# Weight sums of a Strassen feed-forward block moved to VectorE in a pinned order

## The chip, the cores and the metric

The kernel runs on one core of a Trainium2 chip. Its time is the device time of one execution in microseconds (us); the number that counts is the median of several executions. The engines are named as the profile names them: PE is TensorE (PEld its weight loads), DVE is VectorE, ACT is ScalarE, POOL is GpSimd, and SP is SyncE, which here issues the transfers.

## The reference

One step of a small two-layer transformer is computed for 128 prompt rows and 512 sample rows of width 1024. Each layer has a feed-forward block, a mixer (attention in layer 0, a Fourier transform with a projection in layer 1) and a second feed-forward block. Each of the three parts normalises the rows, scales and shifts them by vectors computed from a condition, and adds its result, times a gate vector, to the stream.

```python
def _rms(x, g):
    y = xf * lax.rsqrt(jnp.mean(xf * xf, axis=-1, keepdims=True) + EPS)
    return (y * g.astype(jnp.float32)).astype(x.dtype)
def _modulate(h, shift, scale):
    return h * (1 + scale) + shift
def _swiglu(h, wg, wu, wd):                      # 1024 -> 2816 -> 1024
    return (jax.nn.silu(h @ wg) * (h @ wu)) @ wd
...
hs = _modulate(_rms(ys, norm_g[l, 2]), ms[6], ms[7])
ys = ys + 0.5 * ms[8] * _swiglu(hs, ffn_wg[l, 1], ffn_wu[l, 1], ffn_wd[l, 1])
```

## The kernel before, in words

**Arithmetic.** Everything is kept transposed, features on the 128 partitions, the 640 rows along the columns, in two halves: H=0 has 384 columns, H=1 has 256. A matrix product in float32 is made of three products of rounded parts. Each operand is split into a high half (a rounded copy) and a low half (the rest), and `mm3` adds high·high, high·low and low·high (L497, L498 and L499 in the profile). The high half of a weight is cast on ACT, the low half is a subtraction `raw - high`, on POOL (L160 for plain weights, L109 for the sums below).

**Stages.** The change touches the last feed-forward block of the program (`ffn_last`), from about 1860 us on, and the end of the Fourier stage ahead of it. The block runs over six chunks of its hidden features, `CHUNKS = (4, 4, 2, 4, 4, 4)` blocks of 128. In each chunk PE first makes gate and up of each block (one *unit* of weights, 2048 columns, in two transfers of 512 KB), then `down` multiplies the chunk's results `g` by the down weights (one unit for two blocks), 8 output tiles for each column half, and DVE adds each to the stream (L704).

**Strassen units.** Chunk 0 is plain: for each unit, gate and up on H=0 (384 columns), and on H=1. From chunk 1 on the columns are cut into two halves of 320 and a unit is computed by `seven`, seven products instead of eight. They use sums of weights (S1 to S4) and sums of inputs (T1 to T4); the weight sums are made in `load_sums`: DVE adds and subtracts (L124, L125, L128, L133), ACT casts (L113), POOL or DVE makes the low halves (L109). Between products ACT copies partial results out of PSUM (`snap`, L858) and takes a silu (L888), and DVE adds another product (L870, L883, L893) and multiplies gate and up (L862). The products write to two regions `a` and `b` of one PSUM tile, so a product into one also waits for a read of the other. Two units are interleaved; the last of a chunk ends with its products S4 and A22 alone. At the start and the end of the chunk nothing of another unit stands between the products.

**Buffers.** A unit's split weights live in a ring of three (`wpool`), the forms S2 to S4 in a pool of 12, raw weights in a pool of three. A unit's transfer, casts and sums are a small task; tasks advance on virtual time, which the kernel's author counts with `tick` as PE work is emitted. This fixes the order in which instructions are written. In the kernel before, the scheduler of the framework may then reorder each engine's instructions by its own estimate of when they are ready.

**Head of the block.** `PreNorm` normalises the input: squares (ACT), their sum over feature tiles (POOL, L519), a matmul of ones on the sum (L535), the root (POOL, L545), diagonal matrices (DVE, L552) and a matmul that spreads the factor over partitions (L557). Then for each of 8 feature tiles DVE scales (L320), ACT shifts and rounds (L323), and DVE makes the low half (L324). It is done for H=0 and then H=1. The input sums T1 to T4 follow (L342, ACT L352).

Of the kernel before, what the change touches and what calls it, by code (L numbers as in the profile page):

```python
# [21 lines left out]
KT = D // P  # L22
# [52 lines left out]
class Units:  # L75


    def __init__(self, k):
        self.k = k
        self.todo = []  # L80
        self.ready = []
        self.turn = self.served = self.live = 0

# [3 lines left out]
    def prefetch(self, n=1, eng=None):  # L87
        for _ in range(n):
            if self.todo:
                self.ready.append(self.k.spawn(self.load(*self.todo.pop(0), eng or self.k.nc.gpsimd)))  # L90

    def load_sums(self, ap, cols, eng):


        k, nc = self.k, self.k.nc
        W = UNIT // 4
        r1, r2 = k.raw(), k.raw()
# [4 lines left out]
        turn = self.turn  # L102
        self.turn += 1
        forms = {}

        def low(eng, lo, src, hi):
            for o in range(0, src.shape[1], W):
                c = slice(o, o + W)
                eng.tensor_tensor(lo[:, c], src[:, c], hi[:, c].bitcast(F32), op=ALU.subtract)  # L109

        def put(names, src, eng, at=None):
            h, l = (k.wide(k.fpool, "form", w=W) for _ in range(2)) if at is None else (hi[:, at], lo[:, at])
            nc.scalar.copy(h, src)  # L113
            low(eng, l, src, h)
            for n, name in enumerate(names):
                forms[name] = tuple(t[:, n * W : (n + 1) * W] for t in (h, l))

        yield 3500
        while self.served < turn:
            yield 300  # L120
        s1 = k.wide(k.spool2, "s1", F32, W)
        put(("A11", "A12"), r1, eng, slice(0, RAW))
        yield 500
        nc.vector.tensor_tensor(s1, r2[:, :W], r2[:, W:], op=ALU.add)  # L124
        nc.vector.tensor_tensor(r2[:, :W], r1[:, :W], r2[:, :W], op=ALU.subtract)  # L125
        yield 500
        put(("S1",), s1, eng, slice(RAW, RAW + W))
        nc.vector.tensor_tensor(s1, s1, r1[:, :W], op=ALU.subtract)  # L128
        while self.live > 1:
            yield 300  # L130
        self.live += 1
        put(("S2",), s1, nc.vector)
        nc.vector.tensor_tensor(r1[:, W:], r1[:, W:], s1, op=ALU.subtract)  # L133
        yield 700
        put(("S3",), r2[:, :W], nc.vector)
        yield 700
        put(("S4",), r1[:, W:], nc.vector)
        yield 700
        put(("A22",), r2[:, W:], eng, slice(RAW + W, UNIT))
        self.served += 1  # L140
        return forms

    def load(self, ap, cols, eng):
# [6 lines left out]
        for c in range(0, cols, RAW):  # L150
            e = min(RAW, cols - c)
            raw = self.k.raw()
            nc.sync.dma_start(raw[:, :e], ap[:, c : c + e])
            raws.append((raw, c, e))
        for i, (raw, c, e) in enumerate(raws):
            yield 1500 if i else 4000
            nc.scalar.copy(hi[:, c : c + e], raw[:, :e])  # L157
            for o in range(0, e, 512):
                w = min(512, e - o)
                eng.tensor_tensor(  # L160
                    lo[:, c + o : c + o + w],
                    raw[:, o : o + w],
                    hi[:, c + o : c + o + w].bitcast(F32),
                    op=ALU.subtract,
                )
        return hi, lo
# [100 lines left out]
class PreNorm:  # L267


    def __init__(self, k, l, i):  # L270
        self.k, self.l, self.i = k, l, i
        self.h = []
        self.acc = [None, None]
        self.task = [None, None]
        self.feeds = [None, None]
        self.open = self.free = False
        self.started = False
        self.pauses = [(2500, 3000), (9000, 3000)]
# [25 lines left out]
    def normalise(self, H):  # L304
# [4 lines left out]
        sh, sc = (k.mod[self.l][3 * self.i + j] for j in range(2))  # L309
        for d in range(KT):  # L310
            while not self.open:
                yield 200
# [4 lines left out]
            x = k.xs(d, H)  # L317
            for cols, c in k.parts(H):
                b = sh[:, d, c : c + 1]
                nc.vector.scalar_tensor_tensor(  # L320
                    t[:, cols], x[:, cols], sc[:, d, c : c + 1], r[:, cols], ALU.mult, ALU.mult
                )
# [3 lines left out]
                )  # L326
            yield 900
# [56 lines left out]
class Kern:  # L384
# [74 lines left out]
    def open_last(self):  # L459
# [4 lines left out]
        self.open_halves(8, 3, "right")  # L464
# [431 lines left out]

    def ffn_last(self, l, i, nrm, nxt, before_last):
# [5 lines left out]
        for ch, nf in enumerate(CHUNKS):  # L903
# [14 lines left out]
            else:  # L918
                gs = wide(nf)
# [20 lines left out]
            if last:  # L940
                before_last()
            for H in (0, 1) if ch == 0 or last else ("second", "first"):
# [4 lines left out]
            u.prefetch(nf // 2)  # L947
# [397 lines left out]
    def fourier(self, nrm, nxt):  # L1345
# [120 lines left out]
        def out(w, q, H):  # L1466
            n = NA if H == 0 else NB
            for j in range(2):
# [10 lines left out]
                self.add_x(ps, 2 * q + j, H, gate, nxt if H == 0 else None)  # L1479
# [13 lines left out]
        nxt.later(1)  # L1493
# [362 lines left out]
```

## Time and profile before

| what | before |
|---|---|
| median of 3 runs | 2390.07 us (2389.2 to 2391.84) |
| profiled execution, its own time | 2390.42 us |
| its span in the trace | 2388.6 us |
| mean granted PE clock | 0.983 |
| PE / DVE / ACT / POOL busy | 96% / 67% / 34% / 40% |

The span is what the trace covers; 1.8 us of the profiled execution's time lie outside it. PE is the engine that is nearly always busy. "Granted clock" is the share of the full TensorE clock that PE was given; it has two levels, 1.2 and 2.4 GHz, so that 0.50 is the lower one and a mean between says how long each held.

### The profile page before, as it was taken

What the parts mean: (1) busy time and instruction counts of PE and PEld (TensorE: products, weight loads), DVE (VectorE), ACT (ScalarE), POOL (GpSimd) and SP (SyncE); (2) the same over time, 40 slices, a digit from 0 to 9 for tenths busy, and PEclk for the clock granted to TensorE, in tenths of its full rate; (3) what the DMA queues carried; (4) which work ended last, traced back from release to release, by engine and by line L of the source; (5) the groups of instructions that cost most, each with busy time, mean ns of one, the idle gap of its engine ahead of it and who ended that gap; (6) DMA issues with size and microseconds to landing.
All of it is one profiled execution on the core that took longest, in us unless ns stands there. A gap on an engine that the chain in (4) does not pass through costs nothing. (4 is left out here: it accounts for less than half of the span.)

```text
span 2388.6 us, 38803 instructions
## 1 busy us (share of the span) xinstructions
PE 2291.5 (96%) x15518; PEld 2255.8 (94%) x15518; DVE 1595.8 (67%) x2984; ACT 815.7 (34%) x1689; POOL 947.6 (40%) x763
## 2 busy tenths in 40 slices
PE   8899999999999999999999999999999898989988
PEld 6899999998999999999999999999999798988988
DVE  5877778777777886677767767765364565465554
ACT  4222222254544522222225222222273324232433
POOL 1534433464111443343436334433355334334423
PEclk9999999999999999999999999999999799999999
DMA  8544434321111243333442443432211122121221
GB/s 297 164 133 133 150 123 143 126 75 48 41 41 45 89 132 123 126 122 117 147 137 73 132 124 124 135 121 78 67 61 55 54 71 73 54 86 54 89 71 53
DMA packets 70467, 243.90 MB, mean 102 GB/s; under 512 B 7888, under 2 KB 12688, under 8 KB 70032
## 3 DMA queue, kind: packets, MB, share of 16 engines
q1 hardware_dynamic: 70288, 241.44, 31.7%
q8 instruction: 122, 2.00, 0.3%
q14 instruction: 57, 0.47, 0.1%
HBM read 238.62 MB, written 2.79 MB: 101 GB/s over the span
## 5 line engine op out<-in xcount | busy, mean ns | idle before, releaser
L160 POOL TENSOR_TENSOR wlo<-raw,whi 128x512 fp32r<-128x512 f32 (+1 forms) x520 | 736.2, 1446 | 1081.5 <-ACT whi L157 1034.2
L157 ACT CAST whi<-raw 128x1024 fp32r<-128x1024 f32 (+1 forms) x267 | 269.7, 1036 | 515.3 <-PE t L498 244.9
L704 DVE SCALAR_TENSOR_TENSOR x<-t,mod,x 128x128 f32<-128x128 f32 (+3 forms) x696 | 277.1, 433 | 152.0 <-PE t L499 149.7
L613 DVE CUSTOM_DVE_ANT_0 junk<-wmt,crow 128x1024 f32<-128x1024 f32 x256 | 372.7, 1456 | 3.1 <-ACT crow L1580 0.6
L497 PE MATMUL s<-a,whi 128*128 128x386 f32 (+1 forms) x1056 | 359.7, 341 | 5.4 <-DVE b L740 3.4
L499 PE MATMUL s<-a,wlo 128*128 128x386 f32 (+1 forms) x1056 | 359.8, 341 | 0.1
L498 PE MATMUL s<-a,whi 128*128 128x386 f32 (+1 forms) x1056 | 358.7, 340 | 0.0
L497 PE MATMUL s<-b,whi 128*128 128x256 f32 (+1 forms) x1056 | 296.6, 281 | 0.0
L499 PE MATMUL s<-b,wlo 128*128 128x256 f32 (+1 forms) x1056 | 296.4, 281 | 0.0
L498 PE MATMUL s<-b,whi 128*128 128x256 f32 (+1 forms) x1056 | 296.4, 281 | 0.0
L497 PE MATMUL t<-a,whi 128*128 128x384 f32 (+1 forms) x792 | 270.6, 342 | 14.5 <-DVE x L704 5.3
L498 PE MATMUL t<-a,whi 128*128 128x384 f32 (+1 forms) x792 | 269.3, 340 | 0.9 <-DVE a L507 0.7
L499 PE MATMUL t<-a,wlo 128*128 128x384 f32 (+1 forms) x792 | 268.1, 339 | 0.0
L497 PE MATMUL t<-b,whi 128*128 128x256 f32 x760 | 215.4, 283 | 4.8 <-ACT b L563 2.7
L498 PE MATMUL t<-b,whi 128*128 128x256 f32 x760 | 213.8, 281 | 0.0
L499 PE MATMUL t<-b,wlo 128*128 128x256 f32 x760 | 213.8, 281 | 0.0
L497 PEld LDWEIGHTS s<-a,whi 128*128 128x128 f32 x1056 | 200.4, 190 | 6.6 <-issue 4.2
L499 PEld LDWEIGHTS s<-a,wlo 128*128 128x128 f32 x1056 | 200.2, 190 | 2.3 <-issue 1.6
L498 PEld LDWEIGHTS s<-a,whi 128*128 128x128 f32 x1056 | 200.2, 190 | 1.6 <-issue 1.2
L497 PEld LDWEIGHTS s<-b,whi 128*128 128x128 f32 x1056 | 199.1, 189 | 0.0
L498 PEld LDWEIGHTS s<-b,whi 128*128 128x128 f32 x1056 | 198.9, 188 | 0.0
L499 PEld LDWEIGHTS s<-b,wlo 128*128 128x128 f32 x1056 | 198.8, 188 | 0.0
(294 smaller groups left out, 4868.7 us busy)
## 6 DMA issues: line engine op xcount, KB each, us to landing
raw<-in_gu SPq DMA_DIRECT2D x176, 512.0 KB, 3.7
wmt<-in_wm SPq DMA_DIRECT2D x134, 512.0 KB, 3.7
raw<-in_dn SPq DMA_DIRECT2D x88, 512.0 KB, 3.7
raw<-in_uq SPq DMA_DIRECT2D x8, 512.0 KB, 3.7
raw<-in_wo SPq DMA_DIRECT2D x8, 512.0 KB, 3.7
raw<-in_fw SPq DMA_DIRECT2D x8, 512.0 KB, 3.8
crow<-in_wm SPq DMA_DIRECT2D x6, 512.0 KB, 6.0
junk<-in_wm SPq DMA_DIRECT2D x4, 512.0 KB, 5.5
```

Source lines behind the costliest of these rows:

```text
L157: nc.scalar.copy(hi[:, c : c + e], raw[:, :e])
L160: eng.tensor_tensor(lo[:, c + o : c + o + w], raw[:, o : o + w], hi[:, c + o : c + o + w].bitcast(F32), op=ALU.subtract,)
L497: mm(out, wh, xh, start=first and i == 0, stop=False)
L498: mm(out, wh, xl, start=False, stop=False)
L499: mm(out, wl, xh, start=False, stop=last and i == end)
L613: nc.vector.tensor_tensor_reduce(self.junk, raw, self.crow[:, c * D : (c + 1) * D], 1.0, 0.0, ALU.mult, ALU.add, self.mod[l][m][:, d, c : ...
L704: self.mark = self.nc.vector.scalar_tensor_tensor(xd, ps[:, cols], gate[:, d, c : c + 1], xd, ALU.mult, ALU.add)
```

## The change

Nothing changes before the end of the Fourier stage. There and after it:

- **Order.** `pin` adds dependencies without semaphores between successive instructions of PE, DVE and ACT, from chunk 1 on, except in the last `down`. These engines then take their instructions in the order in which the kernel writes them.
- **Weight sums.** `load_sums` is cut into five steps, 1900 units of virtual time apart, each with less work. From chunk 1 on every low half is made on DVE (L120 and L177 of the new kernel), one instruction of 1024 columns for A11 and A12; POOL has none left there. One further raw buffer (`raws`) is taken, and seven and two scratch tiles of the column halves remain instead of eight and three.
- **Turns.** The down units' loads get a turn in the same row as the sums, so that they wait for the unit ahead of them. One unit less is in flight after chunk 0.
- **Head.** In the Fourier stage's `out` the squares of H=1 are made tile by tile as for H=0, and no longer in a task behind it. The pauses before the normalisation of H=1 are shorter. The scaling of a tile is written two tiles ahead of its use.

```diff
@@ Units.load_sums
+        tt = nc.vector.tensor_tensor
+        def high(name, src, at=None): ... nc.scalar.copy(forms[name][0], src)
+        def low(name, src):
+            h, l = forms[name]
+            tt(l, src, h.bitcast(F32), op=ALU.subtract)
-        put(("A11", "A12"), r1, eng, slice(0, RAW))
-        yield 500
-        nc.vector.tensor_tensor(s1, r2[:, :W], r2[:, W:], op=ALU.add)
...
+        tt(s1, r2[:, :W], r2[:, W:], op=ALU.add)
+        high("A11A12", r1, slice(0, RAW))
+        yield self.pace
+        low("A11A12", r1)
+        high("S1", s1, slice(RAW, RAW + W))
+        high("A22", r2[:, W:], slice(RAW + W, UNIT))
+        yield self.pace
+        low("S1", s1)
+        tt(s1, s1, r1[:, :W], op=ALU.subtract)
+        tt(r2[:, :W], r1[:, :W], r2[:, :W], op=ALU.subtract)
+        yield self.pace
...
+        tt(r1[:, W:], r1[:, W:], s1, op=ALU.subtract)
+        high("S2", s1)
+        high("S3", r2[:, :W])
+        yield self.pace
+        low("S2", s1)
+        low("S3", r2[:, :W])
+        high("S4", r1[:, W:])
+        yield self.pace
+        low("A22", r2[:, W:])
+        low("S4", r1[:, W:])
@@ Units.load
+        turn = self.take_turn() if self.turn else None
+        if turn:
+            yield 3000
+            while self.served < turn:
+                yield 300
@@ PreNorm
-        self.pauses = [(2500, 3000), (9000, 3000)]
+        self.pauses = [(2500, 2000), (6000, 3000)]
...
+        scaled(0)
+        yield 400
+        scaled(1)
...
+            if d + 2 < KT:
+                scaled(d + 2)
@@ ffn_last
+                if ch == 1:
+                    u.eng = self.nc.vector
+                    self.pin(True)
...
+            if ch:
+                self.pin()
             for H in (0, 1) if ch == 0 or last else ("second", "first"):
                 self.down(wds, g, H, gate, nxt if last else None)
-            u.prefetch(nf // 2)
+            elif not last:
+                self.pin()
+            u.prefetch(nf // 2 - (ch == 0))
@@ fourier
-                self.add_x(ps, 2 * q + j, H, gate, nxt if H == 0 else None)
+                self.add_x(ps, 2 * q + j, H, gate, nxt)
-        nxt.later(1)
+        nxt.finish(1)
```

The line numbers of the new kernel are higher: L525 to L527 are the three products, L120 and L177 the low halves, L126, L134, L135 and L140 the sums, L886 the snap, L890, L898, L911 and L921 DVE's additions and products, L916 the silu, L732 the addition to the stream, L332 and L349 the scaling and the low half of the normalisation, L369 the input sums, L547 the sum of squares.

On POOL, at the head of the block, the six additions to the squares' sum `b` of H=1 stand, before the change, behind the low halves of three units (`wlo`, each row two instructions) and ahead of the root (L545):

```order
L160 TENSOR_TENSOR wlo_19721<-raw_19722,whi_19720 128x512 x2
L160 TENSOR_TENSOR wlo_19721<-raw_19724,whi_19720 128x512 x2
L160 TENSOR_TENSOR wlo_19793<-raw_19794,whi_19792 128x512 x2
L160 TENSOR_TENSOR wlo_19793<-raw_19796,whi_19792 128x512 x2
L519 TENSOR_TENSOR b_19941<-b_19941,b_19949 128x256
L519 TENSOR_TENSOR b_19941<-b_19941,b_19955 128x256
L519 TENSOR_TENSOR b_19941<-b_19941,b_19961 128x256
L519 TENSOR_TENSOR b_19941<-b_19941,b_19967 128x256
L519 TENSOR_TENSOR b_19941<-b_19941,b_19973 128x256
L519 TENSOR_TENSOR b_19941<-b_19941,b_19979 128x256
L545 TENSOR_TENSOR rstd_20063<-sm_20061,mhalf 128x2
```

After it, the first two of the six additions stand above this piece, the other four between the low halves of the first two units, and the third unit's are behind the last of them:

```order
L177 TENSOR_TENSOR wlo_19460<-raw_19461,whi_19459 128x512 x2
L177 TENSOR_TENSOR wlo_19460<-raw_19463,whi_19459 128x512 x2
L547 TENSOR_TENSOR b_19425<-b_19425,b_19734 128x256
L547 TENSOR_TENSOR b_19425<-b_19425,b_19773 128x256
L177 TENSOR_TENSOR wlo_19738<-raw_19739,whi_19737 128x512 x2
L177 TENSOR_TENSOR wlo_19738<-raw_19741,whi_19737 128x512
L547 TENSOR_TENSOR b_19425<-b_19425,b_19808 128x256
L177 TENSOR_TENSOR wlo_19738<-raw_19741,whi_19737 128x512
L547 TENSOR_TENSOR b_19425<-b_19425,b_19849 128x256
L177 TENSOR_TENSOR wlo_19812<-raw_19813,whi_19811 128x512 x2
L177 TENSOR_TENSOR wlo_19812<-raw_19815,whi_19811 128x512 x2
L573 TENSOR_TENSOR rstd_20018<-sm_20016,mhalf 128x2
```

On DVE, in chunk 0, the normalisation of H=1 before the change. `s` and `t` are its two scaled tiles (L320), `h` the low halves (L324), and the input sums (L342) and the products of gate and up (L835, L507) stand between them:

```order
L835 TENSOR_TENSOR a_20017<-s_19937,a_20017 128x384
L507 TENSOR_TENSOR g_19894<-a_20017,g_19893 128x384
L342 TENSOR_TENSOR a_20201<-h_19897,h_19898 128x320
L320 SCALAR_TENSOR_TENSOR s_20089<-x_75,mod_7_108,s_20089 128x128
L835 TENSOR_TENSOR a_20084<-s_20022,a_20084 128x384
L324 SCALAR_TENSOR_TENSOR h_19898<-s_20089,mod_6_107,h_19897 128x128
L320 SCALAR_TENSOR_TENSOR s_20089<-x_75,mod_7_108,s_20089 128x128
L507 TENSOR_TENSOR g_19896<-a_20084,g_19895 128x384
L324 SCALAR_TENSOR_TENSOR h_19898<-s_20089,mod_6_107,h_19897 128x128
L320 SCALAR_TENSOR_TENSOR t_20092<-x_76,mod_7_108,s_20089 128x128
```

After it, two tiles are scaled first, each with two instructions, and their low halves follow together; the first input sum (L369) comes behind the third and fourth tile's scaling:

```order
L535 TENSOR_TENSOR g_19921<-a_20029,g_19920 128x384
L332 SCALAR_TENSOR_TENSOR s_20054<-x_75,mod_7_108,s_20054 128x128 x2
L332 SCALAR_TENSOR_TENSOR t_20057<-x_76,mod_7_108,s_20054 128x128 x2
L349 SCALAR_TENSOR_TENSOR h_19925<-s_20054,mod_6_107,h_19924 128x128
L349 SCALAR_TENSOR_TENSOR h_19930<-t_20057,mod_6_107,h_19929 128x128
L349 SCALAR_TENSOR_TENSOR h_19925<-s_20054,mod_6_107,h_19924 128x128
L349 SCALAR_TENSOR_TENSOR h_19930<-t_20057,mod_6_107,h_19929 128x128
L332 SCALAR_TENSOR_TENSOR s_20054<-x_77,mod_7_108,s_20054 128x128 x2
L332 SCALAR_TENSOR_TENSOR t_20057<-x_78,mod_7_108,s_20054 128x128 x2
L349 SCALAR_TENSOR_TENSOR h_19935<-s_20054,mod_6_107,h_19934 128x128
L349 SCALAR_TENSOR_TENSOR h_19940<-t_20057,mod_6_107,h_19939 128x128
L369 TENSOR_TENSOR a_20204<-h_19924,h_19925 128x320
```

On DVE, at the end of chunk 1, before the change: the last unit's additions (L883, L862, L507, L893), then `down`'s additions to the stream (L704), with the next unit's sums (L124, L125, L128) between:

```order
L883 TENSOR_TENSOR a_21375<-s_21262,a_21375 128x320
L124 TENSOR_TENSOR s_3114_21381<-raw_21346 128x512
L125 TENSOR_TENSOR raw_21346<-raw_21345,raw_21346 128x512
L862 TENSOR_TENSOR a_21396<-a_21375,a_21396 128x320
L507 TENSOR_TENSOR g_20916<-a_21396,g_20915 128x320
L893 TENSOR_TENSOR a_21327<-s_21262,a_21327 128x320
L704 SCALAR_TENSOR_TENSOR x_75<-t_21435,mod_8_109,x_75 128x192
L862 TENSOR_TENSOR a_21279<-a_21327,a_21279 128x320
L704 SCALAR_TENSOR_TENSOR x_75<-t_21435,mod_8_109,x_75 128x128
L704 SCALAR_TENSOR_TENSOR x_76<-t_21456,mod_8_109,x_76 128x192
L704 SCALAR_TENSOR_TENSOR x_76<-t_21456,mod_8_109,x_76 128x128
```

After it: the same additions of the last unit, and then the four low halves (L177) of the chunk's second down unit, `wlo_21333`, ahead of the first addition to the stream. The first down unit's low halves stand seven rows further up:

```order
L911 TENSOR_TENSOR a_21362<-s_21249,a_21362 128x320
L890 TENSOR_TENSOR a_21377<-a_21362,a_21377 128x320
L535 TENSOR_TENSOR g_20911<-a_21377,g_20910 128x320
L921 TENSOR_TENSOR a_21314<-s_21249,a_21314 128x320
L890 TENSOR_TENSOR a_21263<-a_21314,a_21263 128x320
L535 TENSOR_TENSOR g_20911<-a_21263,g_20910 128x320
L177 TENSOR_TENSOR wlo_21333<-raw_21334,whi_21332 128x512 x2
L177 TENSOR_TENSOR wlo_21333<-raw_21336,whi_21332 128x512 x2
L732 SCALAR_TENSOR_TENSOR x_75<-t_21410,mod_8_109,x_75 128x192
L732 SCALAR_TENSOR_TENSOR x_75<-t_21410,mod_8_109,x_75 128x128
```

On PE the matmuls of `down` that use this second unit are the third and the fourth block's, six of the first tile's twelve.

## Rows read from the trace of the kernel before

**Rows 1.** Page: busy us of each engine, share of the span, instructions.

```profile
PE 2291.5 (96%) x15518; PEld 2255.8 (94%) x15518; DVE 1595.8 (67%) x2984; ACT 815.7 (34%) x1689; POOL 947.6 (40%) x763
```

**Rows 2.** Windows by stage: length, busy time of PE, PEld, DVE, ACT, POOL, then PEclk, DMA.

```profile
1700.00:1800.00 100.00, 99.29 (x735) 98.52 (x734) 57.87 (x123) 58.94 (x166) 49.22 (x53) 1.00 0.18 56
1865.00:1906.00 41.00, 31.06 (x138) 27.96 (x137) 22.56 (x64) 13.69 (x34) 6.24 (x8) 0.72 0.07 25
1906.00:1965.00 59.00, 56.42 (x365) 56.09 (x365) 38.23 (x68) 18.36 (x34) 22.93 (x16) 0.96 0.23 72
1965.00:2346.00 381.00, 345.32 (x2247) 338.12 (x2247) 213.53 (x347) 132.60 (x243) 141.69 (x104) 0.96 0.21 68
```

**Rows 3.** Waits of PE, 1860 to 2346 us: total us, times, longest.

```profile
PE s L497 <- ACT a L858: 18.3, 4, 5.2
PE s L497 <- DVE a L883: 10.3, 5, 2.4
PE t L497 <- DVE x L704: 5.9, 6, 2.6
PE s L497 <- ACT h L323: 5.3, 6, 2.0
PE t L535 <- POOL b L519: 4.5, 1, 4.5
```

**Rows 4.** Timeline of POOL and DVE at the head: start, us, idle before and releaser.

```profile
1861.18 5.04 POOL L160 TENSOR_TENSOR wlo<-raw,whi 128x512 fp32r<-128x512 f32 x4 [0.74 <-ACT whi L157]
1866.18 4.75 POOL L519 TENSOR_TENSOR b<-b,b 128x256 f32<-128x256 f32 x6
...
1886.68 0.35 DVE L320 SCALAR_TENSOR_TENSOR s<-x,mod,s 128x128 f32<-128x128 f32 x1 [5.56 <-PE s L557]
...
1889.17 0.49 DVE L342 TENSOR_TENSOR a<-h,h 128x320 f32<-128x320 f32 x1
```

**Rows 5.** Timeline of four engines at the start of chunk 1, 1972 to 1984 us.

```profile
1972.40 1.05 ACT L113 CAST whi<-raw 128x1024 fp32r<-128x1024 f32 x1 [19.30 <-PE t L499]
1973.53 2.54 POOL L109 TENSOR_TENSOR wlo<-raw,whi 128x512 fp32r<-128x512 f32 x2 [22.67 <-ACT whi L113]
1976.01 1.30 POOL L109 TENSOR_TENSOR wlo<-s,whi 128x512 fp32r<-128x512 f32 x1
1977.34 1.76 DVE L128 TENSOR_TENSOR s<-s,raw 128x512 f32<-128x512 f32 x1 [3.63 <-POOL wlo L109]
1979.13 0.62 ACT L113 CAST form<-s 128x512 fp32r<-128x512 f32 x1 [3.37 <-DVE s L128]
...
1983.26 0.41 ACT L858 COPY a<-s 128x320 f32<-128x320 f32 x1
1983.72 0.63 PE L497 MATMUL s<-sum,form 128*128 128x320 f32 x1 [4.79 <-ACT a L858]
```

**Rows 6.** Windows of 3 us around two PE waits.

```profile
1979.00:1982.00 3.00, 0.00 (x0) 0.00 (x0) 2.96 (x3) 1.75 (x3) 2.90 (x2) 1.00 0.00 0
1982.00:1985.00 3.00, 1.28 (x5) 1.29 (x6) 2.05 (x4) 0.78 (x2) 0.00 (x0) 0.52 0.09 19
1985.00:1988.00 3.00, 3.00 (x13) 3.00 (x13) 0.26 (x1) 0.27 (x1) 0.00 (x0) 0.50 0.95 300
2007.00:2010.00 3.00, 2.76 (x19) 2.76 (x20) 1.32 (x4) 1.49 (x4) 0.00 (x0) 1.00 0.33 101
```

**Rows 7.** Lines by form, 1965 to 2346 us: busy us, mean ns, idle before, releaser.

```profile
L109 POOL TENSOR_TENSOR wlo<-raw,whi 128x512 fp32r<-128x512 f32 x51 | 70.3, 1397 | 183.3 <-ACT whi L113 172.2 <-DVE a L862 11.1
L128 DVE TENSOR_TENSOR s<-s,raw 128x512 f32<-128x512 f32 x17 | 24.6, 1447 | 31.2 <-POOL wlo L109 31.2
L109 DVE TENSOR_TENSOR form<-raw,form 128x512 fp32r<-128x512 f32 x34 | 23.8, 702 | 9.9 <-ACT form L113 9.9
L862 DVE TENSOR_TENSOR a<-a,a 128x320 f32<-128x320 f32 x34 | 22.8, 672 | 8.8 <-ACT a L888 8.4
L858 ACT COPY a<-s 128x320 f32<-128x320 f32 x54 | 22.7, 423 | 24.4 <-PE s L499 24.3
```

More of the change, by code (lines that the diff above doesn't have):

```diff
@@ L82, in __init__ @@
         self.turn = self.served = self.live = 0
+        self.pace = 1900
+        self.eng = self.k.nc.gpsimd
     def add(self, ap, cols=UNIT):
@@ L89, in prefetch, with take_turn @@
             if self.todo:
-                self.ready.append(self.k.spawn(self.load(*self.todo.pop(0), eng or self.k.nc.gpsimd)))
+                self.ready.append(self.k.spawn(self.load(*self.todo.pop(0), eng or self.eng)))
+    def take_turn(self):
+        self.turn += 1
+        return self.turn - 1
     def load_sums(self, ap, cols, eng):
@@ L96, in load_sums @@
         W = UNIT // 4
-        r1, r2 = k.raw(), k.raw()
+        turn = self.take_turn()
+        r1 = k.raw()
+        r2 = k.wide(k.rawpool, "raw", F32, RAW) if turn % 2 else k.raw()
         nc.sync.dma_start(r1, ap[:, :RAW])
@@ L101, in load_sums, with high @@
         lo = k.wpool.tile([P, UNIT], F32R, tag="wlo", name=k.name("wlo"))
-        turn = self.turn
-        self.turn += 1
         forms = {}
[L106 to L118, printed above, removed]
+        tt = nc.vector.tensor_tensor
+        def high(name, src, at=None):
+            forms[name] = tuple(k.wide(k.fpool, "form", w=W) for _ in range(2)) if at is None else (hi[:, at], lo[:, at])
+            nc.scalar.copy(forms[name][0], src)
+        def low(name, src):
+            h, l = forms[name]
+            tt(l, src, h.bitcast(F32), op=ALU.subtract)
+        yield 4000
         while self.served < turn:
@@ L121, in load_sums @@
         s1 = k.wide(k.spool2, "s1", F32, W)
-        put(("A11", "A12"), r1, eng, slice(0, RAW))
-        yield 500
-        nc.vector.tensor_tensor(s1, r2[:, :W], r2[:, W:], op=ALU.add)
[L125 to L128, printed above, removed]
+        tt(s1, r2[:, :W], r2[:, W:], op=ALU.add)
[9 more added lines that the diff above has]
+        yield self.pace
         while self.live > 1:
@@ L131, in load_sums @@
         self.live += 1
[L132 to L139, printed above, removed]
+        tt(r1[:, W:], r1[:, W:], s1, op=ALU.subtract)
[8 more added lines that the diff above has]
+        low("S4", r1[:, W:])
         self.served += 1
+        h, l = forms["A11A12"]
+        forms["A11"], forms["A12"] = (h[:, :W], l[:, :W]), (h[:, W:], l[:, W:])
         return forms
@@ L165, in load @@
                 )
+        if turn:
+            self.served += 1
         return hi, lo
@@ L309, in normalise, with scaled @@
         sh, sc = (k.mod[self.l][3 * self.i + j] for j in range(2))
+        def scaled(d):
+            for cols, c in k.parts(H):
+                nc.vector.scalar_tensor_tensor(
+                    ts[d % 2][:, cols], k.xs(d, H)[:, cols], sc[:, d, c : c + 1], r[:, cols], ALU.mult, ALU.mult
+                )
+        scaled(0)
+        yield 400
+        scaled(1)
+        while not self.open:
+            yield 200
         for d in range(KT):
-            while not self.open:
-                yield 200
             if not H:
@@ L316, in normalise @@
             t = ts[d % 2]
-            x = k.xs(d, H)
             for cols, c in k.parts(H):
                 b = sh[:, d, c : c + 1]
-                nc.vector.scalar_tensor_tensor(
-                    t[:, cols], x[:, cols], sc[:, d, c : c + 1], r[:, cols], ALU.mult, ALU.mult
-                )
                 nc.scalar.activation(hi[:, cols], t[:, cols], AF.Identity, bias=b)
@@ L463, in open_last @@
         self.gpool = self.open_pool("gpool", 2 * max(CHUNKS), "right")
-        self.open_halves(8, 3, "right")
+        self.open_halves(7, 2, "right")
+        self.rawpool = self.open_pool("raws", 1, "right")
         self.spool2 = self.open_pool("sums", 2, "right")
@@ L895, in seven, with pin @@
         self.tick(self.last)
+    def pin(self, start=False):
+        traced = self.nc.cur_bb.bb.instructions
+        if not start:
+            for i in traced[self.pinned :]:
+                if i.engine in self.order:
+                    prev = self.order[i.engine]
+                    if prev is not None:
+                        self.tc.add_manual_dep(
+                            i,
+                            prev.name,
+                            mybir.DependencyInfo(mybir.DependencyClass.NoSync, mybir.DependencyReason.DATA),
+                            reason="program order",
+                        )
+                    self.order[i.engine] = i
+        else:
+            self.order = {getattr(mybir.EngineType, e): None for e in ("PE", "DVE", "Activation")}
+        self.pinned = len(traced)
     def ffn_last(self, l, i, nrm, nxt, before_last):
```

## The prediction, made before the change was run

> **What bounds the kernel now.** I read the page first. PE is busy for 2291.5 us, 96% of the span [rows 1], so whatever changes the time must remove matmuls (none are removed here), remove PE's idle time, or raise its clock. Where that idle time lies is the next view, the windows by stage. Up to 1800 us PE is full: 99.29 of 100 us at a granted clock of 1.00 [rows 2]. Behind 1865 us it isn't. From 1865 to 1906 (chunk 0's gate and up) it is busy 31.06 of 41 us at a clock of 0.72; from 1906 to 1965 56.42 of 59 at 0.96; in chunks 1 to 5, 1965 to 2346, 345.32 of 381 at 0.96 [rows 2]. That is 9.9, 2.6 and 35.7 us idle. The time lost to the clock is, roughly, busy time by what the clock lacks: 31.06 x 0.28 = 8.7, 56.42 x 0.04 = 2.3 and 345.32 x 0.04 = 13.8 us. In all 73 us; the change can win no more than that, apart from the 43 us of the last `down` behind 2346, which it leaves unpinned.
>
> The waits of PE name what ends each idle time [rows 3]. In the head it is POOL's `b` (4.5 us, once) and ACT's `h` (5.3 us, six times); in the chunks ACT's snap L858 (18.3 us, four times, up to 5.2) and DVE's L883 (10.3, five times, up to 2.4).
>
> The wait of 4.45 in the head: POOL's six additions to `b` run from 1866.18 to 1870.9, straight behind four low halves that began at 1861.18 [rows 4]. Only then can PE make the statistics, and DVE, after 5.56 us of idling, start to normalise H=1 at 1886.68 [rows 4].
>
> The wait of 4.79 at the start of chunk 1, step by step [rows 5]. The cast for the next unit gets its slot in the ring at 1972.40, when `down` lets go of it. POOL makes three low halves to 1977.3. DVE's subtraction L128, in line behind POOL's read, starts at 1977.34 and takes 1.76. ACT's cast of the form follows at 1979.13, the snap for the unit that PE is working on stands behind it and starts at 1983.26, and PE goes on at 1983.72. The snap itself needs 0.41; it is late because of its place in the queue. Four of five chunks start so.
>
> The clock makes such a wait dearer. It is granted 1.00 within the wait, 0.52 and 0.50 in the two stretches of 3 us behind it; from 2007 to 2010, behind one of L883's waits, which are all under 2.4 us [rows 3], it stayed at 1.00 [rows 6].
>
> **The change, part by part.**
>
> *POOL's additions in the head.* Four of the six now stand between the low halves of the first two units, all ahead of the third unit's, which began at 1861.18 [rows 4]. An addition takes 4.75 / 6 = 0.8 us, so the last is done near 1862 to 1863, before PE gets to the statistics at 1866. The 4.5 us go.
>
> *Normalising H=1.* PE's spreading matmuls move 33 matmuls earlier; at 59 / 365 = 0.16 us each [rows 2] that is 5 us. On DVE the scaling (0.35 us [rows 4]) no longer waits for ACT tile by tile, and the input sums (0.49 [rows 4]) stand behind the first four tiles. Of the 5.3 us of waits for `h` I leave 1.4: a product that frees a PSUM tile (L863) stands behind four scalings of 0.35. So 9.9 us idle become 1.4, a gain of 8.5; with no wait near 4 us, I take 3.2 for the 8.7 of the clock, a gain of 5.5. Together -14, with bounds of -8 (only the 4.5 us, and 3.5 of clock) and -17 (nearly all).
>
> *Chunk 0's `down`.* Its wait of 2.6 us for L704 [rows 3] came from DVE standing in line for POOL's low halves. DVE makes these itself now: -2.6, bounds 0 and -4 (the clock too).
>
> *Lows on DVE.* A unit has five halves of 512 columns and one of 1024. A DVE low of 512 takes 0.70, POOL's 1.40 [rows 7]. The 1024 form isn't in the trace: between 0.70 and two of 0.70, and I take 1.3, near the upper end, since it does the work of two. With four sums of 0.70 and seven instructions of 0.4 to 0.67 in `seven` [rows 7], DVE has 4.8 + 2.8 + 3.3 = 11 us per unit, against 84 matmuls of 345.32 / 2247 = 0.154, 12.9 us on PE. That is close. But some sums can be made while `down` runs, where DVE has about 10 us of work in some 30, so over a chunk DVE stays at three quarters.
>
> *The starts of chunks.* POOL is out of the chain and the sums of a chunk's first units are spread over `down`. Nothing makes the snap wait for 5 us; casts of 1.05 and 0.62 [rows 5] still stand ahead of a snap or silu. Walking through the new order with these durations I get waits of 1.4, 0.9, 0, 1.8 and 1.8 in chunks 1 to 5, 5.9 us in all (bounds 0 and 12). Within chunks two products, 24 matmuls or 3.7 us, cover a snap (0.42) and an addition (0.5), so L883's waits go.
>
> *The ends of chunks: new waits.* With PE pinned, no matmul of `down` can slip between the last unit's products. S4 waits for the snap and DVE's addition: 0.42 + 0.48 and some 0.3 of hand-over, 1.2 us. A22 waits for the silu of S4, 0.7. That is 1.9 x 5 = 9.5. And in the four chunks of four units the second down unit's four lows stand on DVE behind the last unit's additions, as the last order shows. From A22's end: two DVE instructions 0.9, ACT's cast of `g` 0.45 (it is of the snap's size, 0.42 [rows 7]), two weight casts of 1.05 [rows 5], two lows of 0.7 [rows 7], and hand-overs of 0.08, the step from cast to POOL in rows 5, four times: some 5.1 us. PE has eleven matmuls of `down` for that, 1.7. So it waits 3.4, four times: 13.8 us.
>
> *Chunks in sum.* 5.9 + 9.5 + 13.8 = 29.2 us of waits in place of 35.7: -6.5 (bounds -24, if the ends cost nearly nothing, and +8, if starts are at their upper bound). The clock: long waits are fewer, and 3.4 us comes in two pieces; 13.8 becomes 9: -5 (0 to -10).
>
> *Transfers.* 512 KB per buffer at 56 to 75 GB/s leave the queue mostly idle (a DMA share of 0.21 [rows 2]); one unit less in flight and one raw buffer more cost nothing as long as a unit's 12.9 us of PE hide its transfer.
>
> Sum: -14 - 2.6 - 6.5 - 5 = -28.1. The profiled execution took 2390.4, 0.35 above the median, so the median comes out near **2362**.
>
> **The rivals.**
>
> *A. The ends cost little.* If the casts and lows of the second down unit are in time, the 13.8 go, and with them perhaps 4 of clock: 2362 - 17.8 = 2344. For it speaks that the raw data are there early; against it the order, in which these rows stand last.
>
> *B. The head keeps half.* While DVE makes input sums, POOL makes low halves of later units. L128, which ran beside POOL, took 1.45 on average; a low of the same shape that ran apart from it 0.70 [rows 7]. Eight lows of POOL at 0.75 each would hold DVE up by 6 us and PE with it, and the clock would stay low: +6 and +4, 2372. Against it: POOL had little to do in this stretch, 6.24 of 41 us [rows 2].
> The Trainium skill ("SBUF — State Buffer", section "Who interferes with whom") says that a VectorE instruction with two SBUF inputs and a GpSimd instruction that reads SBUF block one another, the later one for as long as the first runs. The 1.45 against 0.70 agrees with it.
>
> *C. The pinned order costs more than I see.* A fixed order on three engines turns any late instruction into a wait for all behind it. If starts and ends cost 45 us and not 29 and the clock gains nothing, the time is 2362 + 16 + 5 = 2383.
>
> *D. Slower: DVE sets the pace.* At 11 us per unit, plus 1.4 for a share of down lows, DVE has 12.4 of 12.9 us. If its instructions run at the upper rates (0.67 for an addition, 1.4 for the 1024 form), S4's product waits for L911 in each of 18 units. One product of 1.85 us covers that instruction; from 1.6 us per unit beyond it the whole gain is eaten (18 x 1.6 = 28.8), and at 2 us the time is 2362 + 36 = 2398. Against it: the 0.67 is a mean over times beside POOL, which is gone.
>
> *E. Nothing changes on the chip,* because the scheduler's order was already nearly this. The orders shown contradict it: 2390.
>
> **How the numbers follow.** Forecast 0.60, A 0.15, B 0.10, C 0.08, D 0.05, E 0.02. About 0.2%, 4.8 us, is what a measurement can tell from no change. The forecast, A and B are faster (0.85), C mostly (0.06): 0.91. E and the slow end of C give "same" 0.04, D "slower" 0.05. The bounds stack to 2335 and 2390. The range for 8 in 10 goes from A, 2342, to C, 2384.
>
> **What would show it right or wrong.** Right: in the trace after, no wait of PE for L547; 1865 to 1906 at a clock of 0.9 or more; no wait of 4 us for L886 at a chunk's start; POOL idle from chunk 1 on; waits of 1 to 3.5 us at the first matmuls of `down` that use the second down unit's casts and lows, in chunks 1, 3, 4 and 5. Wrong: waits for L911 in most units, or for a DVE or ACT form in the middle of chunks (D), DVE over 90% busy in gate and up, or waits for a raw transfer.

## The result, and the profile after

The changed kernel takes 2360.49 us (median of 4 runs, 2359.56 to 2363.62) against 2389.64 before: a ratio of 0.988, 95% interval 0.9862 to 0.9897. The forecast was 2362. The profiled execution took 2359.59 us, 30.8 less than the one of before.

Page, busy times, of the changed kernel, whose span is 2357.8 us:

```profile
PE 2279.4 (97%) x15518; PEld 2243.0 (95%) x15518; DVE 1617.9 (69%) x3074; ACT 814.5 (35%) x1689; POOL 801.9 (34%) x655
```

PE's idle time in the span fell from 97.1 to 78.4 us, by 18.7. Its busy time fell by 12.1 for the same 15518 matmuls: that is the clock, and the slow first matmul behind each wait. The windows by stage (columns as in rows 2) show where. PE's matmuls on `g` tell where the stages end: chunk 0's `down` runs from 1940.23 to 1973.07 us before and from 1924.33 to 1952.78 after, and the last `down` ends at 2377.27 and at 2346.30. So the windows of rows 2 don't hold what the prediction calls them: most of 1906 to 1965, up to 1940, is still gate and up of chunk 0. Cut at these ends, the three stages are the head with chunk 0's gate and up, chunk 0's `down`, and chunks 1 to 5 with the last `down`. Before:

```profile
1859.85:1940.23 80.38, 70.02 (x399) 66.00 (x397) 47.28 (x110) 31.15 (x66) 25.80 (x23) 0.85 0.16 51
1940.23:1973.07 32.84, 30.26 (x196) 29.93 (x195) 20.57 (x39) 5.90 (x11) 7.78 (x6) 0.95 0.20 65
1973.07:2377.27 404.20, 368.52 (x2394) 360.75 (x2393) 226.73 (x375) 146.59 (x275) 152.49 (x116) 0.96 0.21 67
```

After:

```profile
1859.77:1924.33 64.56, 60.63 (x399) 59.41 (x398) 50.22 (x110) 26.71 (x58) 23.98 (x20) 0.97 0.23 74
1924.33:1952.78 28.45, 28.45 (x196) 28.45 (x195) 21.46 (x42) 5.99 (x11) 2.43 (x2) 1.00 0.24 75
1952.78:2346.30 393.52, 365.80 (x2394) 355.09 (x2393) 244.69 (x462) 147.30 (x275) 10.87 (x12) 0.99 0.21 68
```

In the first stage PE has 3.9 us idle at a clock of 0.97, where it had 10.4 at 0.85. Chunk 0's `down` is full at 1.00, where 2.6 us were idle at 0.95. In the chunks PE is idle for 27.7 us where it was for 35.7, at 0.99 and not 0.96. The stages are 15.8, 4.4 and 10.7 us shorter. Two windows more show the signs that the prediction named, a clock over 0.9 in the head and no work on POOL in the chunks:

```profile
1865.00:1906.00 41.00, 37.07 (x233) 35.85 (x232) 30.62 (x68) 15.89 (x38) 14.31 (x12) 0.96 0.25 79
1946.00:2324.00 378.00, 350.27 (x2289) 339.77 (x2288) 235.21 (x441) 135.83 (x249) 0.00 (x0) 0.99 0.21 67
```

The waits of PE, 1860 to 2330 us (total, times, longest):

```profile
PE s L525 <- ACT a L886: 8.2, 13, 2.4
PE s L525 <- ACT a L916: 6.1, 7, 1.4
PE t L525 <- ACT whi L174: 5.6, 4, 1.7
PE s L525 <- DVE a L911: 4.3, 4, 1.1
PE s L525 <- DVE a L863: 2.3, 1, 2.3
PE t L527 <- DVE wlo L177: 1.8, 6, 0.4
PE s L525 <- ACT h L348: 1.3, 1, 1.3
```

The four waits of some 5 us for the snap [rows 3] are gone: L886 now stands for 13, the longest of 2.4 us. In their place there are seven waits for the silu (L916), where the kernel before had one (L888, 2.0 us), and waits that it didn't have at all, for the second down unit's cast and low halves (L174, L177). All these kinds can be seen at the end of chunk 1, in the timeline of DVE, PE and ACT:

```profile
2003.83 0.49 DVE L911 TENSOR_TENSOR a<-s,a 128x320 f32<-128x320 f32 x1 [1.45 <-ACT a L886]
2004.38 0.42 PE L525 MATMUL s<-h,form 128*128 128x320 f32 x1 [1.10 <-DVE a L911]
2006.45 0.44 ACT L916 ACTIVATE a<-s 128x320 f32<-128x320 f32 x1 [2.65 <-PE s L527]
2006.94 0.41 PE L525 MATMUL s<-h,whi 128*128 128x320 f32 x1 [0.53 <-ACT a L916]
...
2010.41 1.99 ACT L174 CAST whi<-raw 128x1024 fp32r<-128x1024 f32 x2
2011.49 2.50 DVE L177 TENSOR_TENSOR wlo<-raw,whi 128x512 fp32r<-128x512 f32 x4 [0.45 <-ACT whi L174]
2011.51 0.42 PE L525 MATMUL t<-g,whi 128*128 128x320 f32 x1 [1.66 <-ACT whi L174]
2013.44 0.41 PE L527 MATMUL t<-g,wlo 128*128 128x320 f32 x1 [0.42 <-DVE wlo L177]
```

S4 waits 1.10 for DVE's L911, A22 0.53 for the silu. Then `down` begins, runs six matmuls, and waits 1.66 for the cast that ACT starts at 2010.41, behind the cast of `g` at 2010.05, and 0.42 for the low half.

### The profile page after: what moved, and what is told of

It is laid out like the page before. It is cut to its first block, busy times and chain, and to the rows that moved or that the text cites. A ratio compares the mean times of both kernels' runs of the same rounds, so it can differ in the third digit from the quotient of the medians.

```text
span 2357.8 us, 38714 instructions
## 1 busy us (share of the span) xinstructions
PE 2279.4 (97%) x15518; PEld 2243.0 (95%) x15518; DVE 1617.9 (69%) x3074; ACT 814.5 (35%) x1689; POOL 801.9 (34%) x655
## 4 chain that ended last, share of the span: by engine, by line
PE 83%; DVE 9%; ACT 4%; issue 2%; POOL 1%; DMA 1%; SPq 0%; POOLq 0%; DVEq 0%; ACTq 0%
PE s L525 15%; PE s L526 15%; PE s L527 15%; PE t L525 12%; PE t L527 11%; PE t L526 11%; ACT whi L174 1%; DVE junk L641 1%; DVE x L732 1%; DVE b L778 1%; DMA crow<-in_wm 1%; PE t L1253 1%; PE t L708 0%; ACT p L1201 0%; DVE b L535 0%
## 5 line engine op out<-in xcount | busy, mean ns | idle before, releaser
L177 POOL TENSOR_TENSOR wlo<-raw,whi 128x512 fp32r<-128x512 f32 x484 | 689.9, 1456 | 995.0 <-ACT whi L174 947.7
L174 ACT CAST whi<-raw 128x1024 fp32r<-128x1024 f32 (+1 forms) x267 | 269.9, 1035 | 495.8 <-PE t L526 239.2
L732 DVE SCALAR_TENSOR_TENSOR x<-t,mod,x 128x128 f32<-128x128 f32 (+3 forms) x696 | 277.0, 432 | 156.9 <-PE t L527 154.5
L525 PE MATMUL s<-a,whi 128*128 128x386 f32 (+1 forms) x1056 | 359.9, 341 | 4.5 <-DVE b L768 3.4
L527 PE MATMUL s<-a,wlo 128*128 128x386 f32 (+1 forms) x1056 | 359.8, 341 | 0.2
L525 PE MATMUL s<-b,whi 128*128 128x256 f32 (+1 forms) x1056 | 296.5, 281 | 0.0
L527 PE MATMUL s<-b,wlo 128*128 128x256 f32 (+1 forms) x1056 | 296.4, 281 | 0.0
L525 PE MATMUL t<-a,whi 128*128 128x384 f32 (+1 forms) x792 | 270.1, 342 | 14.6 <-DVE x L732 6.2
L527 PE MATMUL t<-a,wlo 128*128 128x384 f32 (+1 forms) x792 | 267.7, 338 | 0.0
L525 PE MATMUL t<-b,whi 128*128 128x256 f32 x760 | 215.2, 283 | 3.2 <-ACT b L591 1.2
L527 PE MATMUL t<-b,wlo 128*128 128x256 f32 x760 | 213.5, 281 | 0.0
L525 PEld LDWEIGHTS s<-a,whi 128*128 128x128 f32 x1056 | 200.5, 190 | 6.2 <-issue 4.4
L527 PEld LDWEIGHTS s<-a,wlo 128*128 128x128 f32 x1056 | 200.3, 190 | 2.5 <-issue 1.6
L525 PEld LDWEIGHTS s<-b,whi 128*128 128x128 f32 x1056 | 199.1, 189 | 0.0
L527 PEld LDWEIGHTS s<-b,wlo 128*128 128x128 f32 x1056 | 198.8, 188 | 0.0
```

Source lines behind the costliest of these rows:

```text
L177: eng.tensor_tensor(lo[:, c + o : c + o + w], raw[:, o : o + w], hi[:, c + o : c + o + w].bitcast(F32), op=ALU.subtract,)
L525: mm(out, wh, xh, start=first and i == 0, stop=False)
L527: mm(out, wl, xh, start=False, stop=last and i == end)
L732: self.mark = self.nc.vector.scalar_tensor_tensor(xd, ps[:, cols], gate[:, d, c : c + 1], xd, ALU.mult, ALU.add)
```

## The experiments

Each row is a median; the ratios are to runs of the kernel before on the same chip.

| run | what | us | ratio to before, 95% interval |
|---|---|---|---|
| change | all of it | 2360.5 | 0.988 (0.9862 to 0.9897) |
| e1_head | before + head | 2375.1 | 0.9936 (0.9921 to 0.9951) |
| e2_nohead | change − head | 2372.5 | 0.9926 (0.9911 to 0.994) |
| e3_nopin | change − pin | 2323.3 | 0.9718 (0.9704 to 0.9733) |
| e4_pinpool | change, lows on POOL | 2377.5 | 0.9947 (0.993 to 0.9964) |
| e5_lowdve | before + lows on DVE | 2354.7 | 0.9849 (0.9835 to 0.9864) |
| e6_steps_pool | change − pin, lows on POOL | 2389.2 | 0.9989 (0.9979 to 1.0) |
| e7_pin_pe | change, pin on PE alone | 2332.7 | 0.9757 (0.974 to 0.9773) |
| e8_pin_dve_act | change, pin on DVE and ACT | 2334.7 | 0.9764 (0.9749 to 0.9778) |
| e9_head_lows | before + head + lows on DVE | 2325.8 | 0.973 (0.9716 to 0.9745) |
| e10_dn_early | change, down units earlier | 2352.8 | 0.9846 (0.983 to 0.9862) |
| e11_nopin_pause | e3 + shorter pauses | 2320.2 | 0.9708 (0.9692 to 0.9725) |
| e12_pin_onego | change, steps 300 apart | 2376.0 | 0.9933 (0.9916 to 0.9949) |

**The head alone, and all but the head.** e1 puts the edits of `PreNorm` and of the Fourier stage's `out` into the kernel before; e2 takes the same lines out of the change.

```diff
-        self.pauses = [(2500, 3000), (9000, 3000)]
+        self.pauses = [(2500, 2000), (6000, 3000)]
...
+        scaled(0)
...
+            if d + 2 < KT:
+                scaled(d + 2)
...
-        nxt.later(1)
+        nxt.finish(1)
```

> The kernel before with the edits of the head alone (squares of H=1 made tile by tile in the Fourier stage, shorter pauses, scaling two tiles ahead). My theory: the head is worth 14 us by itself (6.3 us of PE waits and some 7 of clock in the two traces), so 2376, between 2372 and 2380, with PE's wait for POOL's sum of squares gone and the clock at 0.9 or more in 1865 to 1906 us. Rival: the time won there is given back at the start of chunk 1, since POOL and DVE are no earlier with the weight sums: 2384 to 2390.

> The changed kernel with the head of the kernel before. My theory: the parts add up, so that 14 us come back: 2374 (2370 to 2378). Rival: head and chunks depend on each other (the paced steps need the earlier start, or hide a late one), and it is under 2366 or over 2382.

The head is worth 14.3 us by e1 and 12.1 by e2. The waits in the chunks stay as in rows 3 (waits of PE, e1; L866 and L891 are its snap and its L883):

```profile
PE s L505 <- ACT a L866: 18.6, 5, 5.2
PE s L505 <- DVE a L891: 10.3, 5, 2.5
```

**Without the pin.**

```diff
     def pin(self, start=False):
+        return
```

> The changed kernel without the pinned order: the scheduler orders PE, DVE and ACT again. My theory: what cost most at the starts of the chunks was POOL in the chain and sums made in one go, which the change takes away in any order; the scheduler fills the ends of the chunks (1.6 us for S4 and A22, 2.1 us for the second down unit, per chunk) but puts some snaps behind casts again: 2356 to 2366. Rival: the order is the cause; without it the waits of 4 to 5 us at the starts return, and the chunks' 10 to 12 us are lost: 2370 to 2376.

Both expectations were wrong: it is 37.2 us faster than the change. The windows' row from 1946 us to the end of its last product, and the longest waits of PE from 1860 us to the last `down`:

```profile
1946.00:2289.00 343.00, 341.09 (x2305) 337.45 (x2306) 234.28 (x446) 136.18 (x252) 1.54 (x2) 1.00 0.23 74
```

```profile
PE s L525 <- ACT h L348: 2.4, 1, 2.4
PE s L525 <- DVE a L863: 2.3, 1, 2.3
PE t L525 <- DVE x L732: 1.5, 1, 1.5
PE t L526 <- DVE g L535: 0.9, 3, 0.4
```

Of 27.7 us idle in the chunks 1.9 are left (343 less 341.09), and 1.5 of these, the wait for L732, end at 1947.00, still in chunk 0's `down`. From the end of that `down` (1955.81) to the end of the last one (2310.87) it is 355.1 us, 38.5 less than in the change: 26.8 less idle and 11.7 less busy. How the ends are filled is seen in PE's timeline at the end of chunk 1:

```profile
2001.66 0.31 PE L525 MATMUL t<-g,whi 128*128 128x320 f32 x1
...
2002.68 0.31 PE L526 MATMUL t<-g,whi 128*128 128x320 f32 x1
2002.92 0.41 PE L525 MATMUL s<-h,form 128*128 128x320 f32 x1
...
2004.79 0.31 PE L527 MATMUL t<-g,wlo 128*128 128x320 f32 x1
...
2005.48 0.42 PE L525 MATMUL s<-h,whi 128*128 128x320 f32 x1
```

Between S1's last matmul and S4 (2002.92) stand eight matmuls of `down` (`t<-g`), the first and the last of them shown, between S4 and A22 (2005.48) four more. They cover what cost 1.10 and 0.53 us in the change.

**Who makes the low halves.** e4 and e6 give A11, A12, S1, A22 and the down weights back to POOL, with and without the pin:

```diff
         def low(name, src):
             h, l = forms[name]
-            tt(l, src, h.bitcast(F32), op=ALU.subtract)
+            on = eng if name in ("A11A12", "S1", "A22") else nc.vector
+            for o in range(0, src.shape[1], W):
+                c = slice(o, o + W)
+                on.tensor_tensor(l[:, c], src[:, c], h[:, c].bitcast(F32), op=ALU.subtract)
...
-                    u.eng = self.nc.vector
```

> The changed kernel with the pinned order and the paced steps, but the low halves of A11, A12, S1, A22 and of the down weights on POOL again, in pieces of 512 columns. My theory: with POOL's 1.3 us pieces in the chain, DVE's sums, each up to 1.76 us beside POOL, come late, and in a fixed order PE waits for all of it: 2370 to 2385. Rival: only the order and the steps matter, and it makes no difference who makes the low halves: 2358 to 2364.

> The changed kernel without the pin and with the low halves of A11, A12, S1, A22 and of the down weights on POOL as before; paced steps, turns and the new head stay. Theory 1 (POOL in the chain costs the time): the head's 14 us stay and the chunks' waits return: 2362 to 2377. Theory 2 (the steps are what matters): 2323 to 2335.

e4 came out as expected. e6 lies outside both ranges, 12 us above that of theory 1. Without the pin, POOL's low halves cost 66 us (2389.2 against 2323.3). PE waits five times for the snap, 27.9 us in all, and the waits of 6 us at the starts show why, here in e6's timeline of chunk 1 (L123 the low halves, L137 and L901 DVE's subtraction and addition, L889 the snap):

```profile
1959.96 1.30 POOL L123 TENSOR_TENSOR wlo<-s,whi 128x512 fp32r<-128x512 f32 x1
1961.20 4.66 POOL L123 TENSOR_TENSOR wlo<-raw,whi 128x512 fp32r<-128x512 f32 x3
1961.29 1.77 DVE L137 TENSOR_TENSOR s<-s,raw 128x512 f32<-128x512 f32 x1 [3.56 <-POOL wlo L123]
1963.09 0.62 ACT L116 CAST form<-s 128x512 fp32r<-128x512 f32 x1 [3.41 <-DVE s L137]
...
1964.66 1.75 DVE L123 TENSOR_TENSOR form<-s,form 128x512 fp32r<-128x512 f32 x1
...
1968.00 0.48 DVE L901 TENSOR_TENSOR a<-t,a 128x320 f32<-128x320 f32 x1
1968.51 0.47 ACT L902 ACTIVATE a<-a 128x320 f32<-128x320 f32 x1 [2.61 <-DVE a L901]
1968.89 0.41 ACT L889 COPY a<-s 128x320 f32<-128x320 f32 x1
1969.35 0.64 PE L528 MATMUL s<-sum,form 128*128 128x320 f32 x1 [6.25 <-ACT a L889]
```

It is the chain of rows 5: POOL's low half, DVE's subtraction at 1.77 beside POOL, the cast, a second subtraction (1.64) and two low halves (1.75 each) on DVE, still beside POOL, and behind them the addition, the silu and the snap for which PE has waited 6.25 us. With the pin the same POOL work costs less, 2377.5, with waits for the snap of at most 4.8 us. At the same place in e4's trace POOL stops at 1958.7 and goes on at 1963.16, behind a cast on ACT, and the instructions of DVE behind its first subtraction take 0.68 to 0.69. So the pin gains 10 to 12 us where POOL makes the low halves (by the ratios, and by the medians), and loses 37 where DVE does.

**The low halves alone.** e5 is the kernel before, and from chunk 1 on:

```diff
-    ... self.load(*self.todo.pop(0), eng or self.k.nc.gpsimd)
+    ... self.load(*self.todo.pop(0), eng or self.eng)
...
+                if ch == 1:
+                    u.eng = self.nc.vector
```

> The kernel before with one edit: from chunk 1 on all low halves on DVE (in its own five-piece form, sums made in one go, no pin, head as before). The run without the pin was 37 us faster than the change, so the lows on DVE and the paced steps together are worth some 51 us with the scheduler's order. Theory 1: POOL's low halves in the chain were all of it (they take 1.3 to 1.4 us each and hold DVE up, which the scheduler's order does not foresee); then this is 2335 to 2347 and no wait over 3 us is left behind 1965. Theory 2: it is the paced steps and turns, which spread the sums over the down matmuls; then the waits of 4 to 5 us at the starts of the chunks stay, and this is 2375 to 2390.

2354.7, neither range, 8 us off that of theory 1 and 20 off that of theory 2. But the waits of PE say which:

```profile
PE s L498 <- ACT a L859: 6.0, 2, 4.8
PE s L498 <- DVE a L884: 2.0, 1, 2.0
```

Of L858's four waits of up to 5.2 one is left, 4.8 us at the start of chunk 1, with one of 1.2 us later and one of L883's. That start belongs to units whose loads were begun in chunk 0, with POOL as their engine: POOL still makes six of their low halves from 1974.45 us on. e9 puts these on DVE too, and adds the head:

```diff
         if cols == "sums":
-            return (yield from self.load_sums(ap, cols, eng))
+            return (yield from self.load_sums(ap, cols, self.k.nc.vector))
```

> The kernel before with the head's edits and all low halves of the weight sums on DVE from the first summed unit on (down units from chunk 1 on); no pin, no paced steps, no turns, buffers as before. Theory 1 (who makes the low halves and the head are all that matters): as fast as the change without its pin, 2320 to 2330. Theory 2 (the paced steps and turns are worth something of their own, though less than I first thought): 2332 to 2345, with waits of over 1 us left at the starts of chunks.

2325.8: its interval and that of e3 overlap, so without the pin the paced steps, turns and the further raw buffer are worth nothing that can be told. Its longest wait in chunks 1 to 5 is one of 1.2 us, for a silu.

**Which engine's order costs.** The set of pinned engines is cut down, here for e7; e8 keeps the other two:

```diff
-            self.order = {... for e in ("PE", "DVE", "Activation")}
+            self.order = {... for e in ("PE",)}
```

> The changed kernel with the pin on PE alone. The pin costs 37 us on three engines. Theory A: it is PE's order, which keeps matmuls of down from filling the ends of the chunks and products of the next unit from filling the starts: 2350 to 2362, with waits for L911, L916 and the second down unit as in the change. Theory B: it is the order of DVE and ACT, where casts and low halves stand ahead of snaps: 2323 to 2335.

> The changed kernel with the pin on DVE and ACT, PE free. Theory A (PE's order costs the time): 2323 to 2337, the ends of the chunks filled with matmuls of down. Theory B (the order of DVE and ACT): 2348 to 2362, with PE waiting for snaps and for the second down unit's low halves.

e7 fell into the range of its theory B, e8 into that of its theory A: each run by itself seems to clear the engines that it pinned, so neither theory holds alone. Either half costs 9 to 11 us over e3's 2323.3, and both together 37: 16 more than their sum. Each half by itself leaves one way out. With PE pinned (waits of PE, e7), DVE and ACT have the second down unit ready in time, and S4 and A22 still wait:

```profile
PE s L525 <- DVE a L911: 4.7, 4, 1.4
PE s L525 <- ACT a L886: 2.9, 5, 0.7
PE s L525 <- ACT a L916: 2.9, 5, 0.8
```

With DVE and ACT pinned (e8), PE fills the ends, and the cast of the second down unit is the wait that it meets most:

```profile
PE t L525 <- ACT whi L174: 4.3, 4, 1.4
```

**The second down unit.**

```diff
-            yield 3000
+            yield 1000
...
-            yield 1500 if i else 4000
+            yield (1000 if i else 500) if turn else (1500 if i else 4000)
```

> The changed kernel, pin and all, with shorter pauses in the down units' loads (1000, 500 and 1000 instead of 3000, 4000 and 1500 of virtual time), so that in the order written the second down unit's casts and low halves stand ahead of the last unit's S4 and A22 additions, or beside them. If the 2.1 us behind each chunk of four (1.66 for the cast, 0.42 for the low halves) are due to that place in the order, PE's waits for L174 and L177 go and the time falls by 5 to 8 us, to 2352 to 2356. Rival: the casts, now ahead of the snaps, make S4 and A22 wait longer by as much: 2358 to 2364.

2352.8, 7.7 less than the change and within the range expected. The waits for L174 and L177 (7.4 us) are gone, but those for the silu doubled (waits of PE, e10, and the longest of them in PE's timeline):

```profile
PE s L525 <- ACT a L916: 12.5, 10, 2.6
PE s L525 <- ACT a L886: 6.4, 10, 2.4
```

```profile
2127.81 0.41 PE L525 MATMUL s<-h,whi 128*128 128x320 f32 x1 [2.57 <-ACT a L916]
```

The rival had new waits, but at another place: S4 and A22 wait as long as in the change, 1.10 and 0.53 us in chunk 1, and the silu's longer waits stand ahead of S4, this one by 6.6 us. The chunks have 25.1 us of idle time and the change's 27.7, so only 2.7 us are won by waits. The rest is clock, 0.995 in the mean of the profiled execution and 0.992 in the change's, and it is not there each time: of the four executions of e10 two took 2350.7 us at 0.994 and 0.995, the other two 2355.0 and 2358.3 at 0.991. So the earlier place by itself is worth less than 7.7; at like clocks e10 and the change differ by some 4 us.

**What the steps are for.** `self.pace = 300` in place of 1900, with the pin:

> The changed kernel, pinned, with the five steps of the weight sums 300 instead of 1900 units of virtual time apart, so that a unit's sums, casts and low halves are written almost in one piece. Without the pin, steps and turns were worth nothing that could be told (2325.8 without them and 2323.3 with them). If they matter only because a pinned engine cannot take a ready instruction ahead of a waiting one, this is slower than the change: 2366 to 2385, with more waits of PE for snaps, silus and L911 in the middle of chunks. Rival: their spacing is of no use under the pin either, since the waits are at the ends of the chunks: 2356 to 2364.

13 to 15.5 us slower than the change (by the ratios, and by the medians), with larger waits of PE for the snap, and for DVE's additions to the stream, which the expectation did not name; those for the silu fell to 2.1 us:

```profile
PE s L525 <- ACT a L886: 11.4, 8, 3.7
PE t L525 <- DVE x L732: 10.4, 4, 3.6
```

The steps matter where the order is pinned; where it isn't, e9 shows nothing that can be told.

**The pauses.** `(6000, 3000)` of e3 becomes `(4000, 2000)`:

> The changed kernel without the pin, and with shorter pauses before the normalisation of H=1 (4000 and 2000 instead of 6000 and 3000). Two waits are left in the head, 2.3 us for L863 and 2.4 for L348. If they come from the spreading matmuls standing late on PE, an earlier place wins 2 to 4 us: 2319 to 2322. If from DVE, which makes input sums between the tiles, nothing changes: 2322 to 2325.

2320.2, 3.1 us or 0.13% less than e3, which is under what a comparison here can tell, and the intervals overlap; but in the trace the wait for L348 is gone, and that for L863 has become two of at most 1.2 us, which fits the place on PE as a part of the cause. It is the fastest version run, 70 us below the kernel before.

## Why the prediction was right, and where not

The forecast of 2362 was right to 1.5 us, and the steps of the sum as follows.

- **Head, −14.** Right: 14.3 and 12.1 by e1 and e2, 15.8 between the two profiles. POOL's wait is gone. Idle time left 3.9 us, not 1.4 (L863 took 2.3 and the tiles' ACT step 1.3 more), so 6.4 were won and not 8.5; busy time fell by 9.4 (70.02 to 60.63), where the prediction had 5.5 for the clock.
- **Chunk 0's `down`, −2.6.** Right: no wait is left. Busy time fell by 1.8 as well, at a clock of 1.00 in place of 0.95, which the prediction had in its bound only.
- **Chunks' waits, 35.7 to 29.2.** 27.7 measured, right in sum by two errors. The ends cost 13.8 (L911 4.3, four silus 2.1, L174 and L177 7.4) and not 23.3: the chain of the second down unit is 4.6 us (2008.8 to 2013.44) and not 5.1, since low halves overlap the second cast, and the last chunk, whose `down` is not pinned, waits 0.6. The starts and insides cost 12.2 (the rest of L886 and L916), twice the 5.9 of my walk; 1.7 are for L732. The upper bound of +8 was added up wrongly: with the starts at 12 the waits are 12 + 9.5 + 13.8 = 35.3, which is 0.4 less than before.
- **Chunks' clock, 13.8 to 9, −5.** The clock rose from 0.96 to 0.99, but PE's busy time fell by 2.7 only (368.52 to 365.80), so less was won than forecast. A matmul behind a wait takes 0.41 us in place of 0.31, and there are 36 waits in the chunks where there were some 20; e3, with next to none, is busy for 354.14 us there. How much of the difference these explain was not settled.
- **Sum.** By stages 15.8, 4.4 and 10.7 were won, 30.8 with the small differences outside them, against 14, 2.6 and 11.5: each is within 2 us of its forecast, though within the stages idle and busy time are off by up to 4.
- **Rivals.** D, DVE as the bound, is refuted: DVE is busy 235.21 of 378 us. The 1024-column low half takes 1.22 (1.3 assumed), the addition L890 0.49 and not 0.67, DVE's subtraction 0.69 in place of 1.45, as the lines of the chunks show, here two of them:

```profile
L120 DVE TENSOR_TENSOR wlo<-raw,whi 128x1024 fp32r<-128x1024 f32 x17 | 20.7, 1219 | 2.9 <-ACT whi L116 2.9
L134 DVE TENSOR_TENSOR s<-s,raw 128x512 f32<-128x512 f32 x17 | 11.8, 691 | 0.6
```

- **B** did not come about, but its mechanism is what the change removes elsewhere: DVE beside POOL at 1.77, alone 0.69. A's expectation that an early second down unit saves 17.8 was too high: 7.7 in e10, and less of it by waits.

What the prediction did not see is how its parts are divided. It costed the pinned order against the order of before, and so as one thing with the low halves. Taken apart, the low halves on DVE win 36 (e5), the head 12 to 14, and the POOL halves that e5 leaves in the first units some 12 to 15 more (what is left of e9's 64.8); then the pin gives back 37.2. So the forecast for the chunks, 11.5 us, came out near the 10.7 measured partly by luck: the low halves were worth some four times as much, and the pin took most of it back. C, "the pinned order costs more than I see", names what happened, but not as it was priced: the starts and ends cost 27.7 us and not its 45, and the loss shows only against a run without the pin.

That the scheduler's order is poor with POOL in the chain and good without is shown (e6 against e3). That it misjudges how long POOL's instructions, or DVE's beside them, take would explain it. No trace shows what the scheduler reckoned with, so this stays open.

## What to carry to other kernels

Where a bundle moves work to another engine and fixes an order as well, run the two apart: here the fixed order won 10 to 12 us while the slow engine was in the chain and lost 37 once it was out. The order fixed on three engines cost 16 us more than the two halves of it added up; with one half free, the other's gaps were partly filled. Look at the ends of loops first, where nothing of the next step stands between dependent instructions. Cut windows at the ends of the work and not at round times, or two of them hold different work. And a sum that comes out right may hold two errors: check its terms one by one against the waits of the trace.

## What was not expected of the hardware

The same wait, at the same place, cost clock in one execution and none in another. At the start of chunk 1 the change and e10 both have PE idle for 2.36 us, ending at 1960.42 and 1960.43. Windows of the change:

```profile
1960.00:1965.00 5.00, 4.58 (x21) 4.58 (x22) 1.23 (x1) 1.41 (x4) 0.00 (x0) 0.66 0.45 177
```

and of e10:

```profile
1960.00:1965.00 5.00, 4.57 (x31) 4.57 (x32) 1.45 (x2) 1.85 (x5) 0.00 (x0) 1.00 0.46 169
```

The granted clock behind the wait was 0.66 in the one, 1.00 in the other, and 21 matmuls ran in place of 31. In the kernel before, waits of 2.13 and 2.02 us (ending at 2007.24 and 2232.80) left it at 1.00, as in rows 6, but ones of 1.97 and 2.43 (ending at 2093.80 and 2127.67) were followed by 0.66 over 5 us. Even within one execution, of e4, two waits of 3.34 us for the same snap were followed by 0.66 (ending at 2203.87) and 1.00 (2298.13). So the prediction's reading, that the short waits cost no clock, doesn't hold, and what a wait of 2 to 3.4 us costs in clock can't be read from its length alone here.
